# Part two's down with four pairs by seven products, its left sides summed earlier, A12's product second

## The chip, the cores and the metric

One core of one Trainium2 chip runs the whole kernel. The metric is the device time of one execution in microseconds. The kernel before takes 1944.5 us (median of three runs, 1944.01 to 1945.11).

## The reference

The input is one sequence of 256 tokens, width 2048, all in float32. One block is computed:

```python
h = h + 0.5 * swiglu(rms_norm(h, ffn1_norm), ffn1_w_gu, ffn1_w_down)
h = h + hybrid_mixer(rms_norm(h, mix_norm), ...)   # gated DeltaNet and stick-breaking heads
h = h + 0.5 * swiglu(rms_norm(h, ffn2_norm), ffn2_w_gu, ffn2_w_down)
gate = sigmoid(rms_norm(h, ple_norm) @ ple_w_gate)
h = h + gate * (p @ ple_w_proj)
return rms_norm(h, final_norm)

def swiglu(x, w_gu, w_down):
    gate, up = split(x @ w_gu)      # each 5632 columns
    return (silu(gate) * up) @ w_down
```

The change concerns the two feed-forward blocks (swiglu), and of these the last product, with w_down: 5632 rows by 2048 columns.

## The kernel before

**Precision.** Every float32 operand is split into a high part (a cast to fp32r, on ScalarE) and a low part (the operand minus the high part, on VectorE). A product is three matmuls: high by high, high by low, low by high. Matmuls have 128 rows of depth and 512 columns. A *pair* is 256 rows of weight by 512 columns, loaded into `raw` in one transfer on SP's queue and split by `weight_pair` (lines 77 and 78). For two row blocks of tokens a pair costs 2 x 2 x 3 = 12 matmuls (lines 550 to 552).

**Stages of a feed-forward block.** The 5632 inner columns are 11 blocks of 512. They are handled in three parts, blocks 0 to 2, 3 to 6 and 7 to 10 (`PARTS`). In each part there is one *group* of work for each block's gate and up (kind "gu", half b = 0 is gate, b = 1 is up, eight pairs each), and then two groups for down (kind "dn", nb = 0 and nb = 2), each for two blocks of 512 output columns and for the rows that this part gave.

**Seven products.** In a group, a number `ns` of the pairs is not multiplied plainly: they are seen as 2 by 2 blocks (tokens by depth on the left, A11 to A22; depth by column half on the right, B11 to B22), and eight block products are replaced by seven. A gate/up group has `NS` = 4 such pairs; down has `NS_DOWN`, line 31: two in part one, three in parts two and three. Each product is `ns` x 3 matmuls (lines 342 to 344) and stands for all pairs at once. The left sides that are sums of A's blocks are made by `halves` (line 423): hi + lo (L456), four short subtractions and additions (L462), and a split into Sh and Sl (L464, L465). The right sides are made in `Group.all_sums` (line 290): each is split into shi and slo (L298, L299) and the four tiles `R` are added into one another between the splits, on VectorE (L307), or by a transfer that reads the other quarter again from memory and adds it (`accum_op`, L314, issued by POOL). The quarters are loaded by POOL as well (L279), the last one, B21, a step after the other three.

The order of the products is `SEVEN` = (0, 1, 2, 4, 3, 5, 6), line 34. Product 0 (A11 by B11) goes to c21, and ScalarE copies it to c11 (L347); product 1 goes to c12 and is copied to c22; product 2 goes on in c21, and ScalarE copies c21 to `part` (L350), which VectorE takes from c12 (L352); product 3 the same with c22; product 4 (A12 by B21) goes on in c11; products 5 and 6 in c12 and c21.

**Order of the work.** The seven products of a group are spread over the plain pairs of the group before it: `plan` (line 354) writes out by hand a list in which, after the second plain pair, one product follows each plain pair. The same list, `order`, says when weights are fetched: `next_weights` (line 85) keeps up to two pairs and one sum ahead of what is being multiplied. The follower's quarters are put in this list two groups ahead. Other work is done in generators, the lanes, of which each advances by one step after every plain pair: lane 0 holds `down_input` (line 475), which turns a finished block of silu(gate) x up into down's left side (multiplication L482, transpose L487, out to memory and back as tT, split L504 and L505); lane 1 holds `halves`. The instructions so written are then placed on each engine by the framework's scheduler, which may put later ones first, unless they are marked to keep their order.

For the down of parts two and three, `halves` starts in the last but one gate/up group, after its sixth product (line 539), one pair at a time. In down's first group (nb = 0) the plain pairs that need the part's last block come last (`sort` in `Group.__init__`); `last` (line 583) is the number of steps that `down_input` then waits before it splits that block.

Of the kernel before, what the change touches and what calls it, by code (L numbers as in the profile page):

```python
# [27 lines left out]


NS = 4  # L30
NS_DOWN = tuple(3 if i1 - i0 == 4 else 2 for i0, i1 in PARTS)


SEVEN = (0, 1, 2, 4, 3, 5, 6)


W_IN_ORDER = (2, 0, 4, 3, 1, 5, 8, 10, 12, 9, 11, 13, 6, 7)
# [9 lines left out]
def block_kernel(ctx, tc, a, out):  # L47
# [200 lines left out]
    class Group:  # L248
# [8 lines left out]
        def __init__(self, kind, part, src, quarters, ns, bank, nb=0):  # L257
            self.kind, self.part, self.src, self.ns, self.nb, self.bank = kind, part, src, ns, nb, bank
            self.quarters, self.raw, self.first = quarters, {}, False
            self.last = part == len(PARTS) - 1  # L260
            self.banks = self.follower = None
            self.plain = [(b, g) for b in range(2) for g in range(ns, len(src[0]))]
            if kind == "dn" and nb == 0:

                self.plain.sort(key=lambda x: x[1] >= len(src[0]) - 2)
            elif kind == "behind":

                self.plain.sort(key=lambda x: x[1] // 2)
            self.sums = self.all_sums()
# [20 lines left out]
        def all_sums(self):  # L290

            fp = current[0]

            def halved(j, b):
                w = self.raw[j, b]
                hi = fp.tile([P, NS, NB], F32R, tag="shi", name="shi", bufs=2)[:, 0:self.ns]
                lo = fp.tile([P, NS, NB], F32R, tag="slo", name="slo", bufs=2)[:, 0:self.ns]
                keep(nc.scalar.copy(hi, w))  # L298
                nc.vector.tensor_tensor(out=lo, in0=w, in1=hi, op=ALU.subtract)  # L299
                return hi, lo  # L300

            def keep(ins):

                return tc.keep_in_program_order(ins) if self.first == "2" else ins

            def add(x, y):
                keep(nc.vector.tensor_tensor(out=self.raw[x], in0=self.raw[x], in1=self.raw[y], op=ALU.add))  # L307

            def add_loaded(x, y):


                if self.first:
                    return add(x, y)
                nc.gpsimd.dma_start(out=self.raw[x], in_=self.quarters[y[1]][y[0]], accum_op=ALU.add)  # L314

            for i in SEVEN:
                ws = halved(*((0, 0), (0, 0), (0, 0), (0, 1), (1, 0), (1, 1), (0, 0))[i])
                if i == 0:
                    add((0, 0), (0, 1))
                    add_loaded((0, 1), (1, 1))  # L320
                elif i == 1:
                    add((0, 0), (1, 1))
                elif i == 2:
                    add_loaded((0, 0), (1, 0))
                yield ws
# [28 lines left out]
    def plan(n):  # L354
# [9 lines left out]
        for p, (i0, i1) in enumerate(PARTS):  # L364
            for i in range(i0, i1):
                plain = PLAIN[n]
                if i < plain:
                    src = [([a[f"w_gu{n}0"][2 * i + b][g] for g in range(KD // 2)], None) for b in range(2)]
                else:
                    src = [sources("w_gu" + n, 2 * (i - plain) + b) for b in range(2)]  # L370
                groups.append(Group("gu", p, [x[0] for x in src], [x[1] for x in src], NS if i >= plain else 0,
                                    len(groups) % 2))
            for nb in (0, 2):
                src = [sources(f"w_down{n}{p}", nb + b) for b in range(2)]
                groups.append(Group("dn", p, [x[0] for x in src], [x[1] for x in src], NS_DOWN[p], len(groups) % 2, nb))
# [47 lines left out]
    def halves(kind, his, los, ns, wait=0, at_once=2):  # L423


        for _ in range(wait):
            yield
# [12 lines left out]

        sides[kind] = side

        for g0 in range(0, ns, at_once):
            n = min(at_once, ns - g0)
            k0 = 2 * (g0 % 2)
            hi, lo = (x[g0 // 2][:, k0:k0 + 2 * n] for x in (his, los))
            keep = lambda ins: ins
            if g0 == 2 and n == 1:

                keep = tc.keep_in_program_order  # L450
                yield
            if n == 2:
                x = fp.tile([P, 2 * NB], F32, tag="sil", name="S")
            else:
                x = act.tile([P, NB], F32, tag="nat", name="S", bufs=4)
            keep(nc.vector.tensor_tensor(out=x, in0=hi.bitcast(F32).rearrange("p k x -> p (k x)"),  # L456
                                         in1=lo.bitcast(F32).rearrange("p k x -> p (k x)"), op=ALU.add))
            xv = x.rearrange("p (g j t y) -> p g j t y", g=n, j=2, t=2)
            a11, a12, a21, a22 = (xv[:, :, j, t, :] for t in range(2) for j in range(2))
            for o, y, z, op in ((a22, a21, a22, ALU.subtract), (a21, a11, a21, ALU.subtract),  # L460
                                (a11, a22, a11, ALU.subtract), (a12, a11, a12, ALU.add)):
                nc.vector.tensor_tensor(out=o, in0=y, in1=z, op=op)  # L462
            sx = [y[:, g0:g0 + n].rearrange("p g j t y -> p (g j t y)") for y in (sh, sl)]
            nc.scalar.copy(sx[0], x)  # L464
            nc.vector.tensor_tensor(out=sx[1], in0=x, in1=sx[0], op=ALU.subtract)  # L465
            if not g0 % 2 + n == 1 or g0 + n == ns:
                yield

    def ffn(n, nT, r, scale, next_norm, stat):
        xs = picker(*nT)  # L470
        late = callable(r)
        with tc.tile_pool(name="ffn", bufs=1) as fp:
            hTh, hTl = [], []

            def down_input(u, sil, th, tl, last):

# [24 lines left out]
                for t in range(2):  # L501
                    hi, lo = (x[:, :, t * P:(t + 1) * P].rearrange("p j (q y) -> p q j y", q=4) for x in (th, tl))
                    tv = tT[:, :, t].rearrange("p q (j y) -> p q j y", j=4)
                    keep(nc.scalar.copy(hi, tv))  # L504
                    keep(nc.vector.tensor_tensor(out=lo, in0=tv, in1=hi, op=ALU.subtract))  # L505

            def gated(g):
                sil = fp.tile([P, 2, NB], F32, tag="sil", name="sil")
# [7 lines left out]
            for group, todo in ffn_plan[n]:  # L516
# [5 lines left out]
                if dn and group.nb and not group.last:  # L522
                    lanes.add(1, halves("gu", *nT, NS))
                elif dn and group.nb and group.follower:
                    lanes.add(1, halves("behind", *nxt, NS_BEHIND, 4))
                elif not dn and group.follower.kind == "dn" and not group.part:
                    lanes.add(1, halves("dn", hTh[i0:], hTl[i0:], NS_DOWN[group.part]))
# [4 lines left out]
                for kind, one in todo:  # L532
                    if kind == "seventh":
                        follower = group.follower
                        follower.product(SEVEN[one])
                        if group.part and not dn and one == 5 and follower.kind == "gu" and \
                                follower.follower.kind == "dn":
                            p = PARTS[group.part][0]
                            lanes.add(1, halves("dn", Later(hTh, p), Later(hTl, p), NS_DOWN[group.part], 0, 1))
                        continue  # L540
                    b, g = one
                    whi, wlo = next_weights()
# [29 lines left out]
                    else:  # L572
# [776 lines left out]
def _layout(i):  # L1349
# [7 lines left out]
    for n in "12":  # L1357
        b = _blocks(f[f"ffn{n}_w_gu"][0])
        nb = DFF // NB
        b = np.stack([b[:nb], b[nb:]], axis=1).reshape(b.shape)  # L1360
        m[f"w_gu{n}0"] = np.ascontiguousarray(b[:2 * PLAIN[n]])
        _parted(m, f"w_gu{n}", b[2 * PLAIN[n]:], NS)
        b = _blocks(f[f"ffn{n}_w_down"][0])
        for p, (i0, i1) in enumerate(PARTS):
            _parted(m, f"w_down{n}{p}", b[:, 2 * i0:2 * i1], NS_DOWN[p])
# [32 lines left out]
```

## Time and profile before

| | before |
|---|---|
| median of 3 runs | 1944.5 us (1944.01 to 1945.11) |
| the profiled execution | 1945.28 us |
| its span in the trace | 1943.6 us |
| TensorE, mean granted clock | 0.999 |
| TensorE busy | 1928.1 us (99%), 8884 matmuls |
| VectorE busy | 1570.4 us (81%) |
| ScalarE busy | 1164.1 us (60%) |
| POOL busy | 148.4 us (8%) |
| moved by DMA | 475.05 MB, mean 244 GB/s |

The span is the time from the first to the last instruction in the trace; the profiled execution's own time has 1.7 us around it. PE is TensorE, PEld its weight loads, DVE VectorE, ACT ScalarE, SP and POOL issue transfers. Matmuls overlap, so the pace of TensorE is read from the distance between the starts of two matmuls and not from the duration of one.

### The profile page before, as it was taken

The page shows a single profiled execution, that of the slowest core. Times are in us where ns is not written, and L with a number is a line of the kernel's source. Part 1 is how long each engine was busy: PE and PEld are TensorE (multiplying, and loading weights), DVE is VectorE, ACT ScalarE, POOL GpSimd, SP SyncE. Part 2 cuts the span into 40 slices and gives each one's busy share as a digit, 9 for nine tenths or more (in the row PEclk, how much of TensorE's full clock was granted, in tenths as well). Part 3 has the DMA queues.
Part 4 walks back from the last instruction along what each step waited for, and adds up shares of the span by engine and source line. Part 5 has one row for each costly group of instructions (what it writes and reads, how often), then busy time and mean ns, then how long its engine had stood idle before and what let it go on. Part 6 is the DMA issues. An engine that isn't in the chain of part 4 may idle for free.

```text
span 1943.6 us, 24163 instructions
## 1 busy us (share of the span) xinstructions
PE 1928.1 (99%) x8884; PEld 1594.0 (82%) x8884; DVE 1570.4 (81%) x1703; ACT 1164.1 (60%) x1362; POOL 148.4 (8%) x226
## 2 busy tenths in 40 slices
PE   9999999999999999999999999999999999999998
PEld 7888888888888888878788888888888888888886
DVE  7879878997789766797856579899888987888865
ACT  6656666666666557664555456566556755657654
POOL 0010110000010000010100000010000100001000
PEclk9999999999999999999999999999999999999999
DMA  8778898888888765556565776788888987989764
GB/s 307 269 236 282 252 293 285 237 288 249 280 285 242 228 218 171 176 169 211 161 213 159 244 283 231 226 281 289 248 275 241 327 264 244 271 237 314 234 214 143
DMA packets 144182, 475.05 MB, mean 244 GB/s; under 512 B 19648, under 2 KB 47296, under 8 KB 129856
## 3 DMA queue, kind: packets, MB, share of 16 engines
q1 hardware_dynamic: 107200, 302.16, 44.4%
q0 software_dynamic: 25920, 160.44, 30.2%
q10 hardware_dynamic: 10944, 10.91, 1.8%
q8 instruction: 69, 1.13, 0.2%
q14 instruction: 49, 0.40, 0.1%
HBM read 451.44 MB, written 22.02 MB: 244 GB/s over the span
## 4 chain that ended last, share of the span: by engine, by line
PE 92%; DVE 5%; DMA 2%; issue 1%; ACT 0%; POOL 0%; SPq 0%; POOLq 0%; DVEq 0%; ACTq 0%
PE d L550 5%; PE d L552 5%; PE d L551 5%; PE u L551 5%; PE u L552 5%; PE u L550 5%; PE g L343 5%; PE g L342 5%; PE g L344 5%; PE g L551 4%; PE g L552 4%; PE pj L112 4%; PE pj L113 4%; PE pj L114 4%; PE g L550 4%; PE d L344 3%
## 5 line engine op out<-in xcount | busy, mean ns | idle before, releaser
L77 ACT CAST whi<-raw 128x1024 fp32r<-128x1024 f32 (+1 forms) x489 | 511.3, 1049 | 401.1 <-PE pj L114 106.6
L78 DVE TENSOR_TENSOR wlo<-raw,whi 128x1024 fp32r<-128x1024 f32 (+1 forms) x489 | 592.0, 1218 | 162.9 <-ACT whi L77 161.8
L299 DVE TENSOR_TENSOR slo<-R,shi 128x2048 fp32r<-128x2048 f32 (+2 forms) x224 | 444.9, 1989 | 132.1 <-ACT shi L298 130.1
L298 ACT CAST shi<-R 128x2048 fp32r<-128x2048 f32 (+2 forms) x224 | 373.9, 1671 | 141.5 <-DVE R L307 62.7
L112 PE MATMUL pj<-whi,nTh 128*128 128x512 f32 x448 | 179.4, 401 | 0.0
L113 PE MATMUL pj<-wlo,nTh 128*128 128x512 f32 x448 | 175.2, 391 | 1.1 <-DVE wlo L78 1.1
L114 PE MATMUL pj<-whi,nTl 128*128 128x512 f32 x448 | 174.9, 390 | 0.0
L550 PE MATMUL d<-whi,hTh 128*128 128x512 f32 x448 | 174.5, 390 | 0.0
L551 PE MATMUL d<-wlo,hTh 128*128 128x512 f32 x448 | 174.4, 389 | 0.0
L552 PE MATMUL d<-whi,hTl 128*128 128x512 f32 x448 | 173.4, 389 | 0.0
L551 PE MATMUL g<-wlo,nTh 128*128 128x512 f32 x400 | 156.6, 391 | 0.6 <-DVE wlo L78 0.6
L552 PE MATMUL g<-whi,nTl 128*128 128x512 f32 x400 | 156.0, 390 | 0.0
L551 PE MATMUL u<-wlo,nTh 128*128 128x512 f32 x400 | 155.8, 389 | 0.2 <-DVE wlo L78 0.2
L552 PE MATMUL u<-whi,nTl 128*128 128x512 f32 x400 | 155.6, 389 | 0.0
L550 PE MATMUL g<-whi,nTh 128*128 128x512 f32 x400 | 155.0, 391 | 0.6 <-ACT nTh L161 0.6
L550 PE MATMUL u<-whi,nTh 128*128 128x512 f32 x400 | 153.4, 389 | 0.0
L307 DVE TENSOR_TENSOR R<-R 128x2048 f32<-128x2048 f32 (+2 forms) x68 | 135.7, 1996 | 0.1
L113 PEld LDWEIGHTS pj<-wlo,nTh 128*128 128x128 f32 x448 | 84.2, 188 | 18.9 <-DVE wlo L78 2.7
L550 PEld LDWEIGHTS d<-whi,hTh 128*128 128x128 f32 x448 | 84.1, 188 | 18.1 <-ACT hTh L504 1.0
L552 PEld LDWEIGHTS d<-whi,hTl 128*128 128x128 f32 x448 | 84.1, 188 | 17.8
L114 PEld LDWEIGHTS pj<-whi,nTl 128*128 128x128 f32 x448 | 84.1, 188 | 17.6
L551 PEld LDWEIGHTS d<-wlo,hTh 128*128 128x128 f32 x448 | 84.1, 188 | 17.4
(332 smaller groups left out, 3447.0 us busy)
## 6 DMA issues: line engine op xcount, KB each, us to landing
raw<-in_w_gu SPq DMA_DIRECT2D x199, 512.0 KB, 5.8
raw<-in_w_down SPq DMA_DIRECT2D x112, 512.0 KB, 6.4
raw<-in_w_in SPq DMA_DIRECT2D x112, 512.0 KB, 3.4
R<-in_w_gu2q POOLq DMA_DIRECT2D x54, 1024.0 KB, 8.6
R<-in_w_gu1q POOLq DMA_DIRECT2D x48, 1024.0 KB, 8.3
raw<-in_w_out SPq DMA_DIRECT2D x32, 512.0 KB, 4.3
tT<-scr SPq DMA_DIRECT2D x22, 512.0 KB, 5.8
R<-in_w_down11q POOLq DMA_DIRECT2D x12, 768.0 KB, 7.0
```

The costliest lines, as they stand in the source:

```text
L77: nc.scalar.copy(hi[:, j, :], raw[:, j, :])
L78: nc.vector.tensor_tensor(out=lo[:, j, :], in0=raw[:, j, :], in1=hi[:, j, :], op=ALU.subtract)
L112: nc.tensor.matmul(outs[t], xh[:, c], whi[:, j, :], start=st, stop=False)
L113: nc.tensor.matmul(outs[t], xh[:, c], wlo[:, j, :], start=False, stop=False)
L114: nc.tensor.matmul(outs[t], xl[:, c], whi[:, j, :], start=False, stop=sp)
L298: keep(nc.scalar.copy(hi, w))
L299: nc.vector.tensor_tensor(out=lo, in0=w, in1=hi, op=ALU.subtract)
L307: keep(nc.vector.tensor_tensor(out=self.raw[x], in0=self.raw[x], in1=self.raw[y], op=ALU.add))
L344: nc.tensor.matmul(out, xl, whi[:, g, :], start=False, stop=sp, skip_group_check=True)
L550: nc.tensor.matmul(out, xh[:, c], whi[:, j, :], start=st, stop=False, skip_group_check=True)
L551: nc.tensor.matmul(out, xh[:, c], wlo[:, j, :], start=False, stop=False, skip_group_check=True)
L552: nc.tensor.matmul(out, xl[:, c], whi[:, j, :], start=False, stop=sp, skip_group_check=True)
```

## The change

Down of part two takes four pairs by seven products in both of its groups; the other parts keep two and three. `NS_DOWN` now has one number for each group, and the weights are laid out in memory accordingly. In the first down group of parts two and three (nb = 0) the products come in the order 0, 4, 1, 2, 3, 5, 6, and B12 is added to B11 by an adding transfer instead of VectorE. The left sides of these groups are made differently: those of pairs one and two are summed in the middle of the last but one gate/up group (`first_sides`, into "nat" tiles) and split after its sixth product; those of the third pair (and, in part two, the fourth) are made in `down_input` straight from tT, when the part's second block arrives, and split one per step in the group after (`later_sides`). `last` falls from 3 to 2 in part two.

```diff
-NS_DOWN = tuple(3 if i1 - i0 == 4 else 2 for i0, i1 in PARTS)
+NS_DOWN = (2, 2), (4, 4), (3, 3)
+SEVEN_DOWN = (0, 4, 1, 2, 3, 5, 6)
...
+            self.seven = SEVEN_DOWN if kind == "dn" and part and nb == 0 else SEVEN
...
-            for i in SEVEN:
+            for i in self.seven:
                 ws = halved(*((0, 0), (0, 0), (0, 0), (0, 1), (1, 0), (1, 1), (0, 0))[i])
                 if i == 0:
-                    add((0, 0), (0, 1))
+                    (add if self.seven is SEVEN else add_loaded)((0, 0), (0, 1))
                     add_loaded((0, 1), (1, 1))
...
+    def split_sums(s, g0, x, keep=lambda ins: ins):
+        n = x.shape[1] // NB
+        hi, lo = (y[:, g0:g0 + n].rearrange("p g j t y -> p (g j t y)") for y in s)
+        keep(nc.scalar.copy(hi, x))
+        keep(nc.vector.tensor_tensor(out=lo, in0=x, in1=hi, op=ALU.subtract))
...
+            def first_sides(p0):
+
+                for _ in range(4):
+                    yield
+                for g in range(2):
+                    x = act.tile([P, NB], F32, tag="nat", name="S", bufs=4)
+                    sum_sides(x, hTh[p0:], hTl[p0:], g)
+                    early.append(x)
+                    yield
+
+            def later_sides(s, made):
+
+                for g, x in made:
+                    yield
+                    split_sums(s, g, x, tc.keep_in_program_order)
...
+                if pending:
+                    s, ns = pending.pop()
+                    made = []
+                    for g in range(2, ns):
+                        x = act.tile([P, NB], F32, tag="nat", name="S", bufs=4)
+                        xv = x.rearrange("p (j t q y) -> p j t q y", j=2, t=2, q=4)
+                        k = 2 * (g - 2)
+                        add_sides([xv[:, j, t] for t in range(2) for j in range(2)],
+                                  [tT[:, :, t, 32 * (k + j):32 * (k + j) + 32] for t in range(2) for j in range(2)],
+                                  keep)
+                        made.append((g, x))
+                    lanes.add(1, later_sides(s, made))
...
+                elif not dn and group.part and group.follower.kind == "gu" and group.follower.follower.kind == "dn":
+                    lanes.add(1, first_sides(i0))
...
-                            lanes.add(1, halves("dn", Later(hTh, p), Later(hTl, p), NS_DOWN[group.part], 0, 1))
+                            lanes.finish(1)
+                            s = left_sides("dn", Later(hTh, p), Later(hTl, p))
+                            for g in range(2):
+                                split_sums(s, g, early.pop(0))
+                            pending.append((s, NS_DOWN[group.part][0]))
...
-                        last = (3 if i1 - i0 == 4 else 2) if len(hTh) == i1 else 0
+                        last = (6 - NS_DOWN[group.part][0] if i1 - i0 == 4 else 2) if len(hTh) == i1 else 0
```

`left_sides` holds what `halves` had of tiles and sides, `add_sides` and `sum_sides` its subtractions and additions.

## Rows read from the trace of the kernel before

**Rows 1.** The page's first part: busy us (share of the span) and instructions of TensorE.

```profile
PE 1928.1 (99%) x8884; PEld 1594.0 (82%) x8884; DVE 1570.4 (81%) x1703; ACT 1164.1 (60%) x1362; POOL 148.4 (8%) x226
```

**Rows 2.** TensorE's waits, whole span: waited for, us in total, times, longest.

```profile
PE vp L1129 <- DVE R L1150: 1.2, 1, 1.2
```

**Rows 3.** 300 to 400 us, TensorE alone: length, busy (matmuls), granted clock, DMA share, GB/s.

```profile
300.00:400.00 100.00, 100.00 (x442) 1.00 0.86 254
```

**Rows 4.** TensorE's timeline (start, duration): first and thirteenth of twelve spacings, 319 to 322 us.

```profile
319.20 0.39 PE L550 MATMUL u<-whi,nTh 128*128 128x512 f32 x1
...
321.92 0.39 PE L342 MATMUL g<-shi,nTh 128*128 128x512 f32 x1
```

**Rows 5.** The same at part two's down: six matmuls from the first to the last.

```profile
352.52 0.62 PE L550 MATMUL g<-whi,nTh 128*128 128x512 f32 x2
...
354.02 0.40 PE L551 MATMUL g<-wlo,nTh 128*128 128x512 f32 x1
```

**Rows 6.** Waits of TensorE's weight loads, 345 to 400 us.

```profile
PEld g L551 <- DVE wlo L78: 0.3, 1, 0.3
```

**Rows 7.** ScalarE's timeline, 318 to 372 us; in brackets the idle time before it.

```profile
358.91 0.62 ACT L464 CAST Sh<-S 128x512 fp32r<-128x512 f32 x1 [5.08 <-DVE S L462]
```

**Rows 8.** Groups by line and shape: busy us, mean ns of one | idle before.

```profile
L78 DVE TENSOR_TENSOR wlo<-raw,whi 128x1024 fp32r<-128x1024 f32 x487 | 590.6, 1220 | 160.2 <-ACT whi L77 159.1
L77 ACT CAST whi<-raw 128x1024 fp32r<-128x1024 f32 x487 | 510.0, 1051 | 398.4 <-PE pj L114 106.6 <-PE d L552 91.5 <-PE u L552 44.0
L299 DVE TENSOR_TENSOR slo<-R,shi 128x2048 fp32r<-128x2048 f32 x133 | 304.4, 2290 | 112.7 <-ACT shi L298 111.9 <-DMA raw<-in_w_gu 0.6
L298 ACT CAST shi<-R 128x2048 fp32r<-128x2048 f32 x133 | 254.3, 1913 | 104.1 <-DVE R L307 53.7 <-PE g L344 27.2 <-PE u L344 21.2
L299 DVE TENSOR_TENSOR slo<-R,shi 128x1536 fp32r<-128x1536 f32 x56 | 97.9, 1754 | 10.3 <-ACT shi L298 10.1
L307 DVE TENSOR_TENSOR R<-R 128x2048 f32<-128x2048 f32 x42 | 95.7, 2280 | 0.1
L307 DVE TENSOR_TENSOR R<-R 128x1536 f32<-128x1536 f32 x16 | 27.9, 1746 | 0.0
```

**Rows 9.** VectorE's timeline, 375 to 400 us.

```profile
396.28 1.22 DVE L456 TENSOR_TENSOR S<-nTh,nTl 128x1024 f32<-128x1024 f32 x1
```

**Rows 10.** Stretches, all engines: length, PE, PEld, DVE, ACT, POOL busy; clock, DMA share, GB/s.

```profile
176.00:216.80 40.80, 40.80 (x181) 33.46 (x180) 38.21 (x32) 24.83 (x22) 3.96 (x6) 1.00 0.87 271
...
343.00:379.00 36.00, 36.00 (x160) 29.57 (x159) 32.49 (x37) 23.09 (x27) 3.07 (x5) 1.00 0.84 256
379.00:420.00 41.00, 41.00 (x182) 33.97 (x181) 39.19 (x38) 26.37 (x25) 4.84 (x7) 1.00 0.93 301
420.00:466.00 46.00, 46.00 (x203) 37.68 (x202) 39.99 (x32) 25.20 (x22) 3.96 (x6) 1.00 0.81 260
```

**Rows 11.** Part two's first product and its copy in the timelines; L347's idle time by releaser.

```profile
348.21 0.39 PE L344 MATMUL d<-shi,hTl 128*128 128x512 f32 x1
...
348.64 0.57 ACT L347 COPY d<-d 128x512 f32<-128x512 f32 x1 [0.94 <-PE d L344]
...
  PE d L344: 5.8, 10
```

**Rows 12.** POOL's timeline, B21 of part two; landing times of all gate/up quarters, block one.

```profile
335.29 0.54 POOL L279 DMA_DIRECT2D R<-in_w_down11q  x1 [4.93 <-DVE slo L299]
...
DMA to landing us min/median/max: 5.1/8.4/12.9
```

**Rows 13.** Part one's last block in the timelines: its multiplication and its cast.

```profile
143.61 1.40 DVE L482 SCALAR_TENSOR_TENSOR sil<-u,rstd,sil 128x512 f32<-128x512 f32 x2
...
161.68 1.14 ACT L504 CAST hTh<-tT 128x512 fp32r<-128x512 f32 x2
```

**Rows 14.** The same of part two.

```profile
375.61 0.75 DVE L482 SCALAR_TENSOR_TENSOR sil<-u,rstd,sil 128x512 f32<-128x512 f32 x1
...
398.06 1.13 ACT L504 CAST hTh<-tT 128x512 fp32r<-128x512 f32 x2
```

More of the change, by code (lines that the diff above doesn't have):

```diff
@@ L373, in plan @@
             for nb in (0, 2):
-                src = [sources(f"w_down{n}{p}", nb + b) for b in range(2)]
-                groups.append(Group("dn", p, [x[0] for x in src], [x[1] for x in src], NS_DOWN[p], len(groups) % 2, nb))
+                src = [sources(f"w_down{n}{p}{nb // 2}", b) for b in range(2)]
+                groups.append(Group("dn", p, [x[0] for x in src], [x[1] for x in src], NS_DOWN[p][nb // 2],
+                                    len(groups) % 2, nb))
         if n == "2":
@@ L421, in block_kernel, with left_sides @@
     order.append(("pair", a["w_pp"][3]))
-    def halves(kind, his, los, ns, wait=0, at_once=2):
-        for _ in range(wait):
-            yield
+    def left_sides(kind, his, los):
         fp = current[0]
@@ L441, in halves @@
         sides[kind] = side
[L443 to L467, printed above, removed]
@@ new lines, in left_sides, with add_sides @@
+        return sh, sl
+    def split_sums(s, g0, x, keep=lambda ins: ins):
[3 more added lines that the diff above has]
+        keep(nc.vector.tensor_tensor(out=lo, in0=x, in1=hi, op=ALU.subtract))
+    def add_sides(x, src, keep=lambda ins: ins):
+        a11, a12, a21, a22 = x
+        b11, b12, b21, b22 = src
+        for o, y, z, op in ((a22, b21, b22, ALU.subtract), (a21, b11, b21, ALU.subtract),
+                            (a11, a22, b11, ALU.subtract), (a12, a11, b12, ALU.add)):
+            keep(nc.vector.tensor_tensor(out=o, in0=y, in1=z, op=op))
@@ new lines, in sum_sides, with halves @@
+    def sum_sides(x, his, los, g0):
+        n = x.shape[1] // NB
+        k0 = 2 * (g0 % 2)
+        hi, lo = (y[g0 // 2][:, k0:k0 + 2 * n].bitcast(F32).rearrange("p k x -> p (k x)") for y in (his, los))
+        nc.vector.tensor_tensor(out=x, in0=hi, in1=lo, op=ALU.add)
+        xv = x.rearrange("p (g j t y) -> p g j t y", g=n, j=2, t=2)
+        xs = [xv[:, :, j, t, :] for t in range(2) for j in range(2)]
+        add_sides(xs, xs)
+    def halves(kind, his, los, ns, wait=0):
+        for _ in range(wait):
+            yield
+        s = left_sides(kind, his, los)
+        for g0 in range(0, ns, 2):
+            x = current[0].tile([P, 2 * NB], F32, tag="sil", name="S")
+            sum_sides(x, his, los, g0)
+            split_sums(s, g0, x)
+            yield
@@ L472, in ffn @@
         with tc.tile_pool(name="ffn", bufs=1) as fp:
-            hTh, hTl = [], []
+            hTh, hTl, early, pending = [], [], [], []
+            def first_sides(p0):
[5 more added lines that the diff above has]
+                    early.append(x)
+                    yield
+            def later_sides(s, made):
+                for g, x in made:
+                    yield
+                    split_sums(s, g, x, tc.keep_in_program_order)
             def down_input(u, sil, th, tl, last):
@@ L525, in ffn @@
                     lanes.add(1, halves("behind", *nxt, NS_BEHIND, 4))
+                elif not dn and group.part and group.follower.kind == "gu" and group.follower.follower.kind == "dn":
+                    lanes.add(1, first_sides(i0))
                 elif not dn and group.follower.kind == "dn" and not group.part:
-                    lanes.add(1, halves("dn", hTh[i0:], hTl[i0:], NS_DOWN[group.part]))
+                    lanes.add(1, halves("dn", hTh[i0:], hTl[i0:], NS_DOWN[group.part][0]))
                 if dn and group.last and nxt is None:
@@ L534, in ffn @@
                         follower = group.follower
-                        follower.product(SEVEN[one])
+                        follower.product(follower.seven[one])
                         if group.part and not dn and one == 5 and follower.kind == "gu" and \
@@ L1364, in _layout @@
         for p, (i0, i1) in enumerate(PARTS):
-            _parted(m, f"w_down{n}{p}", b[:, 2 * i0:2 * i1], NS_DOWN[p])
+            for j in range(2):
+                _parted(m, f"w_down{n}{p}{j}", b[2 * j:2 * j + 2, 2 * i0:2 * i1], NS_DOWN[p][j])
     _parted(m, "w_behind", _blocks(f["ple_w_gate"][0])[0:2], NS_BEHIND)
```

## The prediction

> **What bounds the kernel now.** I read the page first, then the waits, then stretches, then single matmuls. The page shows TensorE busy for 1928.1 us of the span of 1943.6 [rows 1]. A busy TensorE need not be a moving one, so I looked for its waits: the largest that it has by name is 1.2 us, once, in the mixer [rows 2]. In a 100 us stretch inside feed-forward one it is never idle and runs 442 matmuls [rows 3]. Twelve matmuls of 512 columns take 321.92 - 319.20 = 2.72 us, 0.2267 us each, and 100 / 0.2267 is 441: those stretches are a gapless stream at the full granted clock (1.00, the 2.4 GHz level). So the time is the number of matmuls times 0.2267 us, as long as casts, subtractions and loads stay ahead [rows 4].
>
> A small loss stands where the change is put. When down of part two begins, the matmul stream goes from 352.52 to 354.02 with six matmuls, 1.50 us instead of 6 x 0.2267 = 1.36: 0.14 us lost [rows 5], beside a weight-load wait of 0.3 us on VectorE's wlo [rows 6]. The third pair's left side is the late one: ScalarE sits 5.08 us before its Sh cast, for the last of the S subtractions [rows 7]. The same pattern is there four times (parts two and three of both feed-forward blocks).
>
> **The matmuls.** Part two's down goes from three to four pairs by seven products, in two groups (nb 0 and 2) per block, four in all. Per group the seven products grow by one pair, 7 x 3 = 21 matmuls, and two plain pairs of 12 go, 24: net three fewer. 4 x 3 = 12 matmuls at 0.2267 us [rows 4] is **-2.72 us**, on the path, since the stream there is gapless.
>
> The Trainium skill, TensorE: Matmul & The Clock Gate, section Back-to-back issue gap, gives about 131 ns for a sustained load-and-multiply stream at 512 columns, and about 216 ns for the isolated gap. By these the saving would be 1.6 or 2.6 us; the trace's 0.2267 us agrees with neither and decides.
>
> **The stalls at the four starts.** Pairs one and two are now summed in the gate/up group before, while part two's own starting group has the third and fourth made straight from tT, without the hi + lo add. What they cost today is at most 0.3 us each [rows 6] and at least the 0.14 us seen [rows 5]; below that nothing is left to win. I take 4 x 0.14 = **-0.56 us**, bounds -1.2 and 0.
>
> **VectorE and ScalarE.** Per part-two group: two pair splits go (2 x 1.22 us VectorE, 2 x 1.05 ScalarE); seven sums' splits widen by 2.290 - 1.754 = 0.54 us on VectorE; the adds L307 widen by 0.53 us each; at nb 0 of parts two and three one add of 1.75 us goes to a transfer [rows 8]. In down nb 0 of part two VectorE has 39.19 us of work in 41.0; it gets 39.19 - 2.44 + 3.75 + 1.07 = 41.6 us in the 180 matmuls x 0.2267 = 40.8 us that are left. That looks like too much, but some of the 39.19 us is not due there: the next group's nTh sum, L456, already stands at 396.28 in that stretch [rows 9]. In the gate/up group before, VectorE has 32.49 us in 36.0 and gets about 32 in 40.8 (two pairs' sums leave it). In down nb 2 it falls to 39.99 - 2.44 = 37.6 us in 40.8, where part one's down nb 2, the same mix of eight plain pairs and seven four-pair products, carries 38.21 in 40.80 with 181 matmuls, gapless [rows 10]. I cost this at 0: it hides under TensorE. Without that cover it costs up to 1.6 us a block (below).
>
> **A12's product second.** It adds into c11, which ScalarE copies from c21 after the first product, with only one plain pair, 12 matmuls or 2.72 us, between. The same holds for products 2 and 3 now in succession: the part copy must have left c21. The trace has no such neighbours; the nearest row is the present copy: the product's last matmul starts at 348.21 and lasts 0.39, the copy ends 348.64 + 0.57 = 349.21, 0.61 us later. In 10 of 24 cases ScalarE waited for TensorE, otherwise the copy stood behind other casts; behind a four-pair cast and a pair cast it would come 1.91 + 1.05 us later, 3.57 us, 0.85 too late [rows 8, 11]. Bounds 0 and 8 x 0.85 = 6.8 us; I take 0.14 us at each of four groups, the size of the wait seen there, **+0.56 us**. Behind a late copy TensorE's next product and plain pair queue up, nothing else.
>
> A12 also wants B21, the last quarter loaded, two products earlier. It is issued at 335.29; a 1024 KB quarter of gate/up takes 8.4 us to land in the median and 12.9 at most, so it is there at 343.7, or 348.2 [rows 12]. Its cast and subtraction take 1.91 + 2.29 us [rows 8], so ready at 347.9 (352.4 at worst). The first product's nine matmuls, of which the last starts at 348.21, begin at 348.21 - 8 x 0.2267 = 346.40 [rows 11]; with 12 matmuls, then a plain pair, A12's starts at 346.40 + 2 x 2.72 = 351.8. Covered by 3.9 us in the median: 0, at worst 0.6 us a start.
>
> **B11 + B12 by an adding transfer.** The VectorE add was not on the path; the transfer is needed two steps later than the add was, so its 8.4 us [rows 12] end before. POOL issues it behind the first split and ahead of the other adding transfer, which no longer waits for the add. Bytes: the gate/up group moves 256 GB/s x 36.0 us = 9.2 MB; with four wider quarters, a whole quarter and two wider adds, 2.6 MB more, it is 11.8 MB in 40.8 us, 289 GB/s, under the 301 GB/s that the next stretch carries gaplessly [rows 10]. Cost 0.
>
> **The last hidden block.** In part two's down nb 0 only four plain pairs, not six, precede its first use: from the end of gate/up that leaves a product, four pairs and three products, 8 x 2.72 = 21.8 us (28.6 now). In part one, with products of two pairs, only 4 x 2.72 + 4 x 1.36 = 16.3 us stand there; the block was multiplied from 143.61 and cast by 161.68 + 1.14 = 162.8, and the stream around it stayed whole because other work was put first [rows 13]. Cost 0; bound above 1.8 us a block.
>
> **Sum.** -2.72 - 0.56 + 0.56 = -2.7 us. Against the profiled execution (span 1943.6, 1945.28 in all, 0.8 over the median of 1944.5) that is 1942.6; against the median **1941.8 us**.
>
> **The rivals.**
> - *More is won* (0.10): no new wait and all of the 0.3 us at each start back, 1944.5 - 2.7 - 1.2 = 1940.6. For it: sums and adds that leave the crowded start. Against: 0.14 us is all that the stream shows lost.
> - *ScalarE's copies come late* (0.08): both neighbours in all four nb 0 groups wait 0.85 us, 1944.5 - 2.7 + 6.8 = 1948.6, slower than before. It decides where a copy ends over 2.72 us after its product. For it: 14 of 24 copies stood behind casts; against: the 0.61 us seen.
> - *VectorE is the bound in part two's down nb 0* (0.10): 41.6 us of work at a busy share of at most 0.98 is 42.4 us, 1.6 over 40.8, twice: 1945.0. Against: work of the next group done ahead.
> - *The last block is late* (0.08): in part two today the chain from its multiplication, 375.61, to its cast, 398.06 + 1.13 = 399.2, takes 23.6 us [rows 14], 1.8 over 21.8, twice: 1945.4.
> - *The transfers are the bound* (0.04): the Trainium skill, DMA: Bandwidth & Descriptors, section Issuing engines are not separate DMA queues, says that all queues' transfers share the same 16 engines and interleave, so an adding transfer would delay pair loads. By the rows: at no more than the gate/up group's 256 GB/s now, 11.8 MB take 46.1 us, 5.3 over; a lead of two pairs, 5.4 us, hides it when full, and half of it leaves 2.6 us a block: 1947.0. The 301 GB/s of the next stretch speaks against [rows 10].
> - That the change doesn't do what it says: only in that the sooner sums free a VectorE which wasn't binding; the matmuls still go, 1941.8 again.
>
> **How the numbers follow.** The forecast has 0.60, its own range 1941.0 to 1942.8. 0.2% is 3.9 us, about what a measurement here tells from no change. The matmuls alone are 2.7 us, so faster by more needs the first rival nearly whole plus the runs' spread of 0.6 us: 0.12. Slower by over 0.2%, above 1948.4, needs the copies, or two rivals together: 0.08. Within: 0.80. The range goes from 1940.4 (first rival) to 1944.6, up to where the VectorE and last-block rivals are half paid; it leaves out the copies and the full prices.
>
> **What would show it.** Right: 12 fewer matmuls; at the four starts a stream without the 1.50 us for six; Sh casts without the 5 us wait; A12's products without a wait on ScalarE. Wrong: waits of TensorE on L347 or L350's successors in d, on L299 in part two's down, or on L504; fewer than 440 matmuls in a 100 us stretch of parts two and three.

## The result and the profile after

| | before | changed |
|---|---|---|
| median | 1944.52 us (10 runs, 1943.85 to 1945.11) | 1949.46 us (10 runs, 1947.02 to 1951.22) |
| ratio | | 1.0025, 95% interval 1.0015 to 1.0035 |
| the profiled execution, its span | 1945.28, 1943.6 us | 1950.49, 1948.8 us |
| matmuls | 8884 | 8872 |
| moved by DMA | 475.05 MB | 480.81 MB |

The change made the kernel slower by 0.25%; the forecast was 1941.8 us, and the measured time lies above the range. The twelve matmuls are gone (compare [rows 1]):

```profile
PE 1928.1 (99%) x8872; PEld 1592.4 (82%) x8872; DVE 1573.9 (81%) x1697; ACT 1171.4 (60%) x1356; POOL 152.4 (8%) x230
```

What has come is found by TensorE's waits and ScalarE's waits for transfers, both over the whole span of the changed kernel (waited for, us in total, times, longest). In the kernel before, TensorE had no wait in down (d) in this list, and ScalarE none for a quarter of down.

```profile
PE d L346 <- DVE Sl L448: 3.9, 2, 2.0
PE d L344 <- ACT d L349: 1.3, 1, 1.3
...
PE d L345 <- DVE slo L301: 0.9, 4, 0.3
...
ACT shi L300 <- DMA R<-in_w_down210q: 10.5, 2, 8.5
ACT shi L300 <- DMA R<-in_w_down110q: 9.1, 2, 7.1
ACT shi L300 <- DMA R<-in_w_down220q: 3.4, 1, 3.4
ACT shi L300 <- DMA R<-in_w_down120q: 3.1, 1, 3.1
```

Both starts of part two (w_down 11 and 21, nb 0) stop TensorE. Those of part three, with three pairs and the same new order, make ScalarE wait a little, and TensorE not at all. Stretches of TensorE alone (length, busy and matmuls, granted clock, DMA share, GB/s) say how much is lost: first two of the kernel before, then, in the next fence, two of the changed kernel.

```profile
350.00:400.00 50.00, 50.00 (x221) 1.00 0.89 267
...
1485.00:1535.00 50.00, 50.00 (x221) 1.00 0.86 257
```

```profile
350.00:400.00 50.00, 47.77 (x201) 0.97 0.84 266
...
1490.00:1540.00 50.00, 46.48 (x202) 1.00 0.87 270
```

Twenty and nineteen matmuls fewer in 50 us, at 0.2267 us each, are 4.5 and 4.3 us. Less the 2.7 us of the matmuls that went and about half a us at the four old starts, that leaves 5.6 us; the two spans differ by 5.2.

The chain behind the first of them is read backwards. TensorE's timeline of the changed kernel (start, duration, idle before it) shows a hole of 2.33 us between two starts, and then matmuls 0.43 us apart instead of 0.23:

```profile
360.77 0.39 PE L595 MATMUL u<-wlo,nTh 128*128 128x512 f32 x1
363.10 0.50 PE L346 MATMUL d<-shi,Sl 128*128 128x512 f32 x1 [1.94 <-DVE Sl L448]
363.44 0.45 PE L344 MATMUL d<-shi,Sh 128*128 128x512 f32 x1
363.69 0.63 PE L345 MATMUL d<-slo,Sh 128*128 128x512 f32 x1
364.11 0.63 PE L346 MATMUL d<-shi,Sl 128*128 128x512 f32 x1
...
367.08 0.40 PE L595 MATMUL u<-wlo,nTh 128*128 128x512 f32 x1
```

The wait ends with the second of two Sl (362.36 + 0.69 = 363.05), by the program's order that of the fourth pair. VectorE's timeline shows where that stands: behind the split slo of B11 + B12, a pair's wlo, the add L309, the third pair's Sl and another wlo.

```profile
355.08 2.29 DVE L301 TENSOR_TENSOR slo<-R,shi 128x2048 fp32r<-128x2048 f32 x1 [1.46 <-ACT shi L300]
357.29 1.22 DVE L79 TENSOR_TENSOR wlo<-raw,whi 128x1024 fp32r<-128x1024 f32 x1
358.42 2.28 DVE L309 TENSOR_TENSOR R<-R 128x2048 f32<-128x2048 f32 x1
360.62 0.69 DVE L448 TENSOR_TENSOR Sl<-S,Sh 128x512 fp32r<-128x512 f32 x1
361.22 1.22 DVE L79 TENSOR_TENSOR wlo<-raw,whi 128x1024 fp32r<-128x1024 f32 x1
362.36 0.69 DVE L448 TENSOR_TENSOR Sl<-S,Sh 128x512 fp32r<-128x512 f32 x1
```

And that split waited for ScalarE, which had waited twice for a transfer: 7.11 us in front of A12's split (B21), 2.00 us in front of that of B11 + B12.

```profile
346.83 1.91 ACT L300 CAST shi<-R 128x2048 fp32r<-128x2048 f32 x1 [7.11 <-DMA R<-in_w_down110q]
...
353.13 1.91 ACT L300 CAST shi<-R 128x2048 fp32r<-128x2048 f32 x1 [2.00 <-DMA R<-in_w_down110q]
```

POOL's timeline says why. The adding transfer of B22 (L316, 331.77) is issued ahead of the load of B21 (L281, 335.62), and that of B12 comes at 341.71. [rows 12] have B21's issue before, 335.29.

```profile
331.77 0.89 POOL L316 DMA_DIRECT2D R<-in_w_down110q  x1 [2.13 <-DMA R<-in_w_down110q]
335.62 0.56 POOL L281 DMA_DIRECT2D R<-in_w_down110q  x1 [2.97 <-ACT Sh L447]
341.71 0.88 POOL L316 DMA_DIRECT2D R<-in_w_down110q  x1 [5.54 <-issue]
```

Before, POOL's timeline has B22's adding transfer behind that load. It overwrites B12, which VectorE's add of B11 and B12 reads, and that add ended at 339.11 + 1.75 = 340.86 (the bracket names the subtraction behind it):

```profile
339.11 1.75 DVE L307 TENSOR_TENSOR R<-R 128x1536 f32<-128x1536 f32 x1
...
341.16 0.89 POOL L314 DMA_DIRECT2D R<-in_w_down11q  x1 [5.33 <-DVE S L462]
```

The DMA view of single microseconds of the changed kernel gives the time to landing (last column) of its second and third transfer, B21 and B12. Before, B21 took 4.7 us, with 768 KB.

```profile
R<-in_w_down110q POOLq DMA_DIRECT2D x1, 1024.0 KB, 11.1
...
R<-in_w_down110q POOLq DMA_DIRECT2D x1, 1024.0 KB, 11.3
```

So the sum is there at 341.71 + 11.3 = 353.0 us, and everything behind it is late. Three transfers of 1 MB are issued on one queue within 10 us. Stretches of all engines, first before, then changed (busy of PE, PEld, DVE, ACT, POOL; clock, DMA share, GB/s), show a DMA share of 0.68 and then of 1.02, and a VectorE that has gaps:

```profile
340.00:350.00 10.00, 10.00 (x45) 8.27 (x45) 10.00 (x19) 6.24 (x8) 0.89 (x1) 1.00 0.68 150
...
340.00:350.00 10.00, 10.00 (x46) 8.28 (x45) 7.46 (x14) 3.17 (x3) 0.88 (x1) 1.00 1.02 317
```

The lower clock is told by stretches of 2 us (length, busy and matmuls, granted clock):

```profile
362.00:364.00 2.00, 0.90 (x3) 0.91 0.23 35
364.00:366.00 2.00, 2.00 (x6) 0.50 0.99 379
366.00:368.00 2.00, 2.00 (x8) 0.74 0.88 176
```

After TensorE had stood for 2.1 us the granted clock was 0.50 (the 1.2 GHz level). From 363.69 to 367.08 eight matmuls took 3.39 us instead of 1.81: 1.6 us more, three quarters of the hole again. In the second feed-forward block a wait of the same length, 1.98 us, was not followed by it.

### The profile page after: what moved, and what is told of

It reads as the page before. It is cut to its first block, busy times and chain, and to the rows that moved or that the text cites. A ratio compares the mean times of both kernels' runs of the same rounds, so it can differ in the third digit from the quotient of the medians.

```text
span 1948.8 us, 24115 instructions
## 1 busy us (share of the span) xinstructions
PE 1928.1 (99%) x8872; PEld 1592.4 (82%) x8872; DVE 1573.9 (81%) x1697; ACT 1171.4 (60%) x1356; POOL 152.4 (8%) x230
## 2 busy tenths in 40 slices
DMA packets 143605, 480.81 MB, mean 247 GB/s; under 512 B 19584, under 2 KB 47232, under 8 KB 125952
## 4 chain that ended last, share of the span: by engine, by line
PE 86%; DVE 7%; DMA 3%; issue 2%; ACT 1%; POOL 0%; SPq 0%; DVEq 0%; POOLq 0%; ACTq 0%
PE u L596 5%; PE u L595 5%; PE u L594 4%; PE g L345 4%; PE g L346 4%; PE g L344 4%; PE pj L113 4%; PE pj L114 4%; PE pj L115 4%; PE d L596 4%; PE d L595 4%; PE d L594 4%; PE g L595 4%; PE g L596 4%; PE g L594 4%; PE d L346 2%
## 5 line engine op out<-in xcount | busy, mean ns | idle before, releaser
L78 ACT CAST whi<-raw 128x1024 fp32r<-128x1024 f32 (+1 forms) x481 | 504.1, 1052 | 375.1 <-PE pj L115 108.3
L79 DVE TENSOR_TENSOR wlo<-raw,whi 128x1024 fp32r<-128x1024 f32 (+1 forms) x481 | 582.7, 1218 | 156.7 <-ACT whi L78 155.6
L301 DVE TENSOR_TENSOR slo<-R,shi 128x2048 fp32r<-128x2048 f32 (+2 forms) x224 | 460.0, 2056 | 136.3 <-ACT shi L300 134.5
L300 ACT CAST shi<-R 128x2048 fp32r<-128x2048 f32 (+2 forms) x224 | 386.6, 1727 | 175.8 <-DVE R L309 82.5
L594 PE MATMUL d<-whi,hTh 128*128 128x512 f32 x416 | 162.1, 390 | 0.0
L595 PE MATMUL d<-wlo,hTh 128*128 128x512 f32 x416 | 161.9, 389 | 0.0
L596 PE MATMUL d<-whi,hTl 128*128 128x512 f32 x416 | 161.1, 390 | 0.0
L309 DVE TENSOR_TENSOR R<-R 128x2048 f32<-128x2048 f32 (+2 forms) x64 | 132.1, 2064 | 0.3
L113 PEld LDWEIGHTS pj<-whi,nTh 128*128 128x128 f32 x448 | 84.2, 188 | 16.6
L594 PEld LDWEIGHTS d<-whi,hTh 128*128 128x128 f32 x416 | 78.1, 188 | 16.9 <-ACT hTh L530 1.0
L596 PEld LDWEIGHTS d<-whi,hTl 128*128 128x128 f32 x416 | 78.1, 188 | 16.9 <-DVE hTl L531 0.5
```

Source lines behind the costliest of these rows:

```text
L78: nc.scalar.copy(hi[:, j, :], raw[:, j, :])
L79: nc.vector.tensor_tensor(out=lo[:, j, :], in0=raw[:, j, :], in1=hi[:, j, :], op=ALU.subtract)
L113: nc.tensor.matmul(outs[t], xh[:, c], whi[:, j, :], start=st, stop=False)
L594: nc.tensor.matmul(out, xh[:, c], whi[:, j, :], start=st, stop=False, skip_group_check=True)
L595: nc.tensor.matmul(out, xh[:, c], wlo[:, j, :], start=False, stop=False, skip_group_check=True)
L596: nc.tensor.matmul(out, xl[:, c], whi[:, j, :], start=False, stop=sp, skip_group_check=True)
```

## The experiments

Three theories stood at the start. **Late transfers**: B22's adding transfer, set free from VectorE's add, goes ahead of B21 and B12's, and these land late. **A12 second**: B21 is wanted too soon, whatever the transfers do. **Four pairs**: the first down group has too much work with four.

### e1: the old order

```diff
-            self.seven = SEVEN_DOWN if kind == "dn" and part and nb == 0 else SEVEN
+            self.seven = SEVEN
```

> The changed kernel with the old order 0, 1, 2, 4, 3, 5, 6 everywhere, so also with B11 + B12 on VectorE; four pairs and the sooner left sides stay. Crowded transfers (the adding transfer of B22, set free from VectorE's add, goes ahead of B21 on POOL's queue, B21 lands 11 us after its issue and stops ScalarE for 7 us): the adding transfer waits for the add again, B21 is wanted two products later, no DMA wait of ScalarE over 2 us in part two, 1941 to 1944 us. A12 second as such (B21 wanted too soon, whatever the transfers do): also 1941 to 1944. Four pairs in the first group are too much: still over 1947.

Measured 1947.52 us, ratio to before 1.0017 (1.0008 to 1.0026), the changed kernel's being 1.0025. No wait of ScalarE for a quarter is left, yet TensorE stops elsewhere: B11 + B12 is wanted by the second product again, and its split is late behind VectorE's add. TensorE's waits:

```profile
PE d L344 <- ACT shi L300: 3.5, 4, 1.5
```

The time is the one that the third theory expected, and a miss for the other two: with the old order four pairs are late on VectorE. The run doesn't tell late transfers from A12 second, since it takes both away.

### e2: the add on VectorE, A12 second

```diff
-                    (add if self.seven is SEVEN else add_loaded)((0, 0), (0, 1))
+                    add((0, 0), (0, 1))
```

> The changed kernel with B11 + B12 added on VectorE again; A12's product stays second. Crowded transfers: the adding transfer of B22 waits for VectorE's add and goes behind B21, which lands some 5 to 8 us after its issue; ScalarE's waits for a transfer in part two fall from 9.1 us to under 3, no 2 us wait of TensorE, 1941 to 1944 us. A12 second as such: B21 is as late as before the edit, 1948 to 1950. Four pairs too much: over 1947.

Measured 1943.45 us, ratio 0.9995 (0.9987 to 1.0004): 6 us less than the changed kernel, as late transfers wants. B22's adding transfer is held by the add again, B21 lands in 5.0 us. ScalarE's casts of the first sums, from its timeline:

```profile
341.70 1.91 ACT L300 CAST shi<-R 128x2048 fp32r<-128x2048 f32 x1 [0.96 <-DMA R<-in_w_down110q]
350.09 1.92 ACT L300 CAST shi<-R 128x2048 fp32r<-128x2048 f32 x1
```

A12 second as such is no cost that this shows, and four pairs in the first group are not too much under the new order: both theories fall. But the edit moves two transfers at once.

### e3: B22's adding transfer written later

```diff
                     (add if self.seven is SEVEN else add_loaded)((0, 0), (0, 1))
-                    add_loaded((0, 1), (1, 1))
+                    if self.seven is SEVEN:
+                        add_loaded((0, 1), (1, 1))
+                elif i == 4 and self.seven is SEVEN_DOWN:
+                    add_loaded((0, 1), (1, 1))
                 elif i == 1:
```

> The changed kernel, in which only the adding transfer of B22 is issued later, after A12's split (second product) instead of after A11's, in the first down groups of parts two and three. Crowded transfers: B21 and then the adding transfer of B12 have the engines to themselves, B21 lands 5 to 8 us after its issue, ScalarE waits under 2 us, 1941 to 1943 us. A12 second as such: 1948 to 1950. Four pairs too much: over 1947.

Measured 1949.4 us, ratio 1.0026 (1.0017 to 1.0036). This would speak against late transfers, had the edit reached the chip: POOL's timeline shows the transfer where it was, in front of B21's load. The place in the program doesn't hold it; it waits for B12's quarter alone, and the scheduler puts it first.

```profile
332.41 0.89 POOL L316 DMA_DIRECT2D R<-in_w_down110q  x1 [2.07 <-DMA R<-in_w_down110q]
336.32 0.55 POOL L281 DMA_DIRECT2D R<-in_w_down110q  x1 [3.03 <-ACT Sh L450]
```

### e4: three pairs in part two's first group, four in its second

```diff
-NS_DOWN = (2, 2), (4, 4), (3, 3)
+NS_DOWN = (2, 2), (3, 4), (3, 3)
...
-                            pending.append((s, NS_DOWN[group.part][0]))
+                            pending.append((s, NS_DOWN[group.part][1]))
```

> The changed kernel with three pairs in part two's first down group and four in its second (last is 3 again); order and adding transfers stay. Half of the matmuls' saving is left, 1.4 us. Four pairs too much in the first group: no wait, about 1943 us. Crowded transfers: the quarters have 768 KB as in part three, where no wait is seen; ScalarE's wait falls to under 3 us and the time to 1943 to 1945. A12 second as such: B21 is wanted as soon as now, still over 1946.

Measured 1942.26 us, ratio 0.9989 (0.9981 to 0.9998): faster than the kernel before. Stretches of 50 us at the same two places hold 222 and 223 matmuls. B21 and B12's transfer take 7.0 and 8.2 us at 768 KB, ScalarE waits for one 3.4 us in the first feed-forward block and 4.7 in the second, and TensorE doesn't wait. The time is under the range of late transfers and ScalarE's wait over its 3 us; the third theory, with about 1943 us, comes nearest. So the order and the transfers of the change have room at three pairs, as in part three, and none at four.

```profile
350.00:400.00 50.00, 50.00 (x222) 1.00 0.93 292
1500.00:1550.00 50.00, 50.00 (x223) 1.00 0.96 304
```

### e5: B21 loaded third, B22 last

```diff
             use = (0, 0), (0, 1), (1, 1), (1, 0)
+            if self.seven is SEVEN_DOWN:
+                use = (0, 0), (0, 1), (1, 0), (1, 1)
```

> The changed kernel with one edit: in the first down groups of parts two and three B21 is loaded third and B22 last (B22's own quarter is wanted late, its adding transfer reads memory). B21 late (its load shares the engines with B22's adding transfer, lands 11 us after its issue, ScalarE stops for 7 us in front of A12's split, and everything behind it slips): B21 is there some 6 us earlier, no wait of ScalarE before A12's split, no 2 us wait of TensorE, 1941 to 1944 us. B11 + B12 by transfer is what is late (its 11 us before the third product): ScalarE still waits 2 us or more there and TensorE on Sl, 1946 to 1950.

Measured 1950.59 us, ratio 1.0025 (1.0016 to 1.0034). B21's wait is gone, and nothing is won. ScalarE's casts of the first two of the quarters in question:

```profile
341.15 1.91 ACT L302 CAST shi<-R 128x2048 fp32r<-128x2048 f32 x1 [0.76 <-ACT whi L78]
...
353.78 1.91 ACT L302 CAST shi<-R 128x2048 fp32r<-128x2048 f32 x1 [3.94 <-DMA R<-in_w_down110q]
```

B12's adding transfer still lands 11.3 us after its issue, behind B22's two transfers of 10.4 and 11.2 us, and TensorE has its 1.9 us wait on Sl. So with the sum still late, taking away the 7.1 us in front of A12's split, the longest wait in the view at this start, wins nothing. My theory had named the wrong one of the two.

### e6: the adding transfers pinned in POOL's order

```diff
-                nc.gpsimd.dma_start(out=self.raw[x], in_=self.quarters[y[1]][y[0]], accum_op=ALU.add)
+                ins = nc.gpsimd.dma_start(out=self.raw[x], in_=self.quarters[y[1]][y[0]], accum_op=ALU.add)
+                if self.seven is SEVEN_DOWN:
+                    tc.keep_in_program_order(ins)
...
```

with the edit of e3, so that POOL issues B21's load, B12's adding transfer and B22's in this order.

> Run e3 again, with the two adding transfers pinned in POOL's order, so that B22's really goes behind B21's load and behind B12's adding transfer. B21 late by sharing: B21 lands in 5 to 6 us as in e2, ScalarE waits under 2 us before A12's split, 1941 to 1944 us though B11 + B12 is still added by a transfer. B11 + B12 by transfer is what is late: 1946 to 1950.

Measured 1942.82 us, ratio 0.9990 (0.9981 to 0.9998), against 1.0025 for the changed kernel, and the two intervals lie apart: the order of three transfers on one queue is worth 0.35%, 6.8 us. B21 lands in 5.0 us. B12's transfer, issued at 341.67 as in the changed kernel (341.71), lands in 8.0 us and not in 11.3, with B22's close behind it, which takes 14.7. B11 + B12 is cast with no wait for a transfer, 3.4 us sooner than in the changed kernel:

```profile
340.73 1.92 ACT L300 CAST shi<-R 128x2048 fp32r<-128x2048 f32 x1 [1.04 <-DMA R<-in_w_down110q]
...
349.77 1.91 ACT L300 CAST shi<-R 128x2048 fp32r<-128x2048 f32 x1 [0.64 <-DVE wlo L79]
```

VectorE has the same order as before the edit, from that sum's split on all of it 3.4 us sooner; the second Sl stands at 359.00 and not at 362.36, and TensorE's wait of 1.9 us is gone:

```profile
355.06 2.29 DVE L309 TENSOR_TENSOR R<-R 128x2048 f32<-128x2048 f32 x1
...
359.00 0.68 DVE L453 TENSOR_TENSOR Sl<-S,Sh 128x512 fp32r<-128x512 f32 x1
```

Late transfers holds, with B12's in the place of B21's: by e5 B21 sooner changes nothing by itself, by e6 B12's sooner gives all of it back. In e6 B21 is sooner too; B12's alone was not run.

### e7: four pairs and nothing else of the change

```diff
-NS_DOWN = tuple(3 if i1 - i0 == 4 else 2 for i0, i1 in PARTS)
+NS_DOWN = 2, 4, 3
...
-                        last = (3 if i1 - i0 == 4 else 2) if len(hTh) == i1 else 0
+                        last = (6 - NS_DOWN[group.part] if i1 - i0 == 4 else 2) if len(hTh) == i1 else 0
```

The edit is to the kernel before.

> The kernel before with part two's down at four pairs and nothing else of the change (old order, old left sides, last at 2 in part two). If the sooner left sides and the order are what four pairs need: the sums of the third and fourth pair come late on VectorE, TensorE waits over 2 us at each of the two starts, 1946 to 1952 us. If four pairs alone cost nothing: 1941.5 to 1942.5 us.

Measured 1952.25 us, just above the range expected, ratio 1.0040 (1.0027 to 1.0052). TensorE's waits, whole span; at each of the two starts of part two 2.2 us of the first:

```profile
PE d L343 <- DVE slo L299: 4.8, 4, 2.2
PE g L551 <- DVE wlo L78: 2.7, 4, 1.2
```

So the fourth pair does need the rest of the change: VectorE is late in the first group.

### e8: the old order with the adding transfer

```diff
-            self.seven = SEVEN_DOWN if kind == "dn" and part and nb == 0 else SEVEN
+            self.seven = SEVEN
+            self.by_transfer = kind == "dn" and part and nb == 0
...
-                    (add if self.seven is SEVEN else add_loaded)((0, 0), (0, 1))
+                    (add_loaded if self.by_transfer else add)((0, 0), (0, 1))
```

> The changed kernel with the old order but B11 + B12 by the adding transfer: the fourth of two orders by two ways to add. The sum is wanted by the second product, about 5.4 us sooner than in the new order, and its transfer takes 8 to 11 us: TensorE waits several us at each of four starts, the slowest of the four, over 1950 us. If the transfer is no part of the cost: as e1, 1947 to 1948 us.

Measured 1966.97 us, ratio 1.0110 (1.0095 to 1.0126). TensorE's waits:

```profile
PE d L345 <- ACT shi L301: 9.9, 5, 3.8
PE d L346 <- DVE slo L302: 6.7, 6, 1.3
```

With e1, e2 and the changed kernel these are two orders by two ways to add, as ratios: old order 1.0017 with VectorE, 1.0110 with the transfer; new order 0.9995 and 1.0025. The transfer costs in both, and A12 second hides much of it, not all.

### e9: Sl not pinned

```diff
-                    split_sums(s, g, x, tc.keep_in_program_order)
+                    split_sums(s, g, x)
```

> The changed kernel, with the splits of the third and fourth pair's left sides no longer pinned to the program's order: one of the two Sl subtractions then stands ahead of the late split of B11 + B12 on VectorE, the other directly behind the add L309, without a pair's wlo between. If TensorE's 2 us wait comes from Sl standing in VectorE's queue behind the late sum's split and its add: the wait falls to 0.5 us or less a start, and with it the stretch at the lower clock, 1943.5 to 1946 us, though B21 and B11 + B12 land as late as before. If the late transfers hold TensorE themselves (through shi and slo): no change, 1948 to 1950.

Measured 1946.33 us, ratio 1.0011 (1.0002 to 1.0020). Between the two expectations: the wait on Sl fell from 1.9 to 1.3 us at the first start and not to 0.5, 0.7 us on ScalarE's copy came beside it, the granted clock of the stretch stays at 1.00, and the runs lie closer together, 1945.68 to 1947.24. TensorE alone, 350 to 400 us:

```profile
350.00:400.00 50.00, 48.09 (x211) 1.00 0.89 281
```

By the ratios, 0.14 of the 0.35% between the changed kernel and e6, each known to about 0.1%, came of where Sl stood behind the late sum, with the stretch at half clock that followed. The rest is left with the late sum.

### e10: e4 with e6's pins

```diff
-NS_DOWN = (2, 2), (4, 4), (3, 3)
+NS_DOWN = (2, 2), (3, 4), (3, 3)
...
```

> Three pairs and then four in part two's down (as e4), with the adding transfers pinned behind B21 (as e6). B21 and B11 + B12 land sooner; e4 had no wait of TensorE left in the down groups, so this changes nothing: 1942 to 1942.6 us, as e4. If e4 still loses something to late transfers: down to 1941.5.

Measured 1942.04 us, ratio 0.9988 (0.9979 to 0.9997), the lowest here, and the same as e4 within the runs' spread. With three pairs the order of the transfers doesn't matter.

### e12: the change without the fourth pair

```diff
-NS_DOWN = (2, 2), (4, 4), (3, 3)
+NS_DOWN = (2, 2), (3, 3), (3, 3)
```

> The changed kernel with three pairs in part two's down, so the kernel before with the sooner left sides, A12 second and the adding transfer alone. The forecast's term for the four starts: 0.14 us won at each, 0.56 us in all, 1943.9 to 1944.1 us against 1944.5. If the order or the adding transfers cost by themselves at three pairs: over 1945.5.

Measured 1944.08 us, ratio 0.9997 (0.9988 to 1.0006): 0.6 us under the kernel before in the medians, which the interval can't tell from nothing. The wlo wait of the four starts [rows 6] is gone: from 340 to 400 us neither TensorE nor its weight loads have a wait.

### e13: e6 and e9 together

> Both repairs at four pairs: adding transfers pinned behind B21 (e6), Sl not pinned (e9). If what is left of e6's loss is Sl behind L309, 1941.5 to 1942.3 us; if it is the part's last block and the next group's sums, as e6, 1942.5 to 1943.

Measured 1942.94 us, ratio 0.9990 (0.9982 to 0.9999), as e6. What e6 has left is thus not Sl. In part two of the second feed-forward block TensorE waits for the last hidden block, and e6 has the same with 0.74 us. TensorE's timeline of e13:

```profile
1527.56 0.50 PE L601 MATMUL d<-whi,hTl 128*128 128x512 f32 x1 [1.07 <-DVE hTl L536]
```

## Why the prediction was wrong

**The matmuls, -2.72 us: right in number.** 8872 instead of 8884. At three and four pairs (e4), with six of the twelve, 2.2 us are won over the kernel before measured beside it, where 6 x 0.2267 = 1.4 and the four starts' 0.56 make 1.9; the interval, 0.02% to 0.19% or 0.4 to 3.7 us, doesn't tell more. The Trainium skill's figure of about 131 ns a matmul, TensorE: Matmul & The Clock Gate, section Back-to-back issue gap, is seen in no stream here; 0.2267 us is.

**The four starts, -0.56 us: the waits went; the size can't be told.** In the changed kernel the Sh casts of part two's start have no 5 us wait for S and the weight loads no wait for wlo there. e12 gives 0.6 us with an interval from -0.12% to +0.06%.

**The step that failed** is "B11 + B12 by an adding transfer", costed at 0, in three places.
- It took 8.4 us to landing, the median of gate/up's quarters. It was 11.3 us, and 12.4 in the second feed-forward block. The prediction's own bound was 12.9, but it was used for B21 alone. In e6, where the order is the one that the prediction assumed, it was 8.0 and 8.4: the size was right for that order, and the order was not there.
- It said that POOL issues this transfer ahead of the other adding transfer. That one "no longer waits for the add", which the prediction saw, and drew the wrong conclusion from: freed of that late condition, it went ahead of B21's load and so of B12's transfer. A wait that is removed also removes an order.
- The bytes were spread over the 40.8 us of a group, 289 GB/s. Three transfers of 1 MB are issued from 331.77 to 341.71, and from 340 to 350 the engines carry 317 GB/s at a share of 1.02.

The price of that step was the 6.8 us between the changed kernel and e6, by the ratios. With it taken out, e6 stands at 0.9990 of the kernel before, 2.0 us faster; the forecast had 2.7.

**A12 second, +0.56 us.** The neighbour that was priced, ScalarE's copy in front of the next product, did hold TensorE, 1.3 us once, in the second feed-forward block; but there the copy stood behind pair casts that an 8.5 us wait for B21 had held up. In e5 and e6 TensorE has no wait on that copy. B21's landing was forecast at 343.7, 348.2 at worst; it was 335.62 + 11.1 = 346.7.

**VectorE and the last block.** No run shows VectorE as the bound in part two's first down group by its sum of work: from 350 to 400 us e2 and e6 hold 220 matmuls each. The share of at most 0.98 that the prediction reckoned with stands in none of its rows; from 340 to 350 us of the kernel before it is 1.00. The last block, costed at 0 and bounded by 1.8 us a block, waits 0.7 and 1.1 us in e6 and e13, in the second feed-forward block only; e12 has 0.7 there with three pairs. In e6 the stretch from 1500 to 1550 us holds 213 matmuls, against 222 before and 223 in e4: 2.0 us, of which waits for hTl, slo and hTh are named (0.74, 0.17 and 0.15 us). So something is lost at the last block, near the bound and not 0, in one of the two feed-forward blocks; which part of the change makes it late is open, as e12 has some of it with three pairs.

**The rivals.** The nearest is the one with 0.04, transfers as the bound, 1947.0. By the Trainium skill, DMA: Bandwidth & Descriptors, section Issuing engines are not separate DMA queues, transfers of all queues share 16 engines and interleave. The trace agrees: B21's load took 5.0 us in e6 and 11.1 beside the other two. But the rival was priced on the pair loads, and what came late was a sum on which the rest of VectorE's queue stood.

**What had no term at all** is the clock. TensorE's hole of 2.1 us was followed by 1.6 us lost at half clock in the profiled execution. In e5 both holes were followed by it, in e9, with waits of 1.3 and 1.4 us, neither. It may be what spreads the changed kernel's runs (4.2 us, against 1.4 for e4): in e5 the mean granted clock of an execution is 0.997 in four of the five slowest and 0.998 in the other seven. But 3.4 us at half clock lower that mean by 0.0009, no more than the last place of these figures, so this is not shown.

## What to carry to other kernels

When an instruction that made others wait is removed, look up what it held back besides its own readers: on a queue, the transfer set free may go ahead of one that is wanted sooner, and its place in the program does not hold it. Cost a transfer from the ones in flight beside it, not from a median or a mean over the stage. The longest wait in a view need not be the one that costs: here taking away the 7.1 us in front of A12's split won nothing by itself, since a sum that came a little later, with a wait of 2.0 us, held up VectorE's queue.

## What was not expected of the hardware

After a stop of 2.1 us TensorE was granted 0.50 of its clock for 3.4 us at one start of the changed kernel, and after a stop as long at the other start of the same execution it was not. Where it was, the stop cost three quarters of its length again.

1 MB transfers that POOL issued within 10 us of each other took 9.9, 11.1 and 11.3 us to land in the first feed-forward block, and 11.9, 12.5 and 12.4 in the second, where B21's load with no other quarter in flight took 5.0 (e6). Sent close behind each other in e6, the first of two landed in 8.0 us and the second in 14.7; sent 4 and 6 us apart in the changed kernel, the first had no such lead.
